# Attention's reciprocals turned with its maxima and spread over partitions by way of DRAM, in a hybrid encoder block

## The chip, the cores and the metric

The kernel runs on one core of a Trainium2 chip. The core has five engines with a queue of instructions each: TensorE (PE; its weight loads are listed as PEld), VectorE (DVE), ScalarE (ACT), GpSimd (POOL) and SyncE (SP), which here issues most DMAs. Each queue is worked off in order. The metric is the device time of one execution in microseconds, the median of the runs.

## The reference

One layer of an encoder over 2048 positions of width 1024, in float32:

```
h = rms_norm(x);  z = h @ W_in                       # 8 gated-MLP heads, 8 attention heads of 64
A = u * (W_s @ layer_norm(v) + b)                    # in blocks of 128 positions, masked
s = q @ k.T / 8 + c[t] - c[s],  s <= t               # c: running sum of log sigmoid(forget logits)
B = softmax(s) @ v                                   # per head
x = x + concat(A, B) @ W_out
x = x + (silu(conv(g)) * conv(val)) @ W_down         # [g, val] = rms_norm(x) @ W_up, causal width 3
out = rms_norm(x)
```

## The kernel before, in words

A float32 product is made of three products in the float32r type: each operand is split into a high and a low part, and high by high, high by low and low by high are summed in one PSUM bank (`mm3`, lines 203 to 213). These dense matmuls, 512 columns wide, are most of the work.

**Attention** runs as a generator beside them (`b_stream`, lines 684 to 703). It goes through four blocks of 512 queries (`tb`), and in each through eight heads (`h`). For one head there are two passes.

- `b_max` (lines 732 to 790) makes the scores of 128 queries by 512 keys (L752, L753), takes their maxima (L756, L758) and, with ScalarE, the sums of the exponentials (L761). At its end DVE makes the maximum over all keys, split in two parts (`m8`, 128 queries x 8: four groups of queries by high and low), and the reciprocals of the sums (`rr`, 128 x 4, L780 or L782).
- Its inner function `turn` (lines 784 to 788) turns `m8` on PE into 8 rows of 128 queries (L786), and DVE writes them, each in its own place by a mask of ones and zeros (`rowsel`), into rows 96 to 103 of the query tile `t1` (L787). With those rows in the product the second pass subtracts the maximum inside the matmul.
- `b_mix` (lines 792 to 851) makes the scores once more, now with the keys on partitions (L813, L814), their exponentials (L819), the split of those (L824, L825), and their product with the values (L801, L802) into one PSUM bank `o`. The two parts of the result are added into `op` (L836, L837), which holds an even head on partitions 0 to 63 and the odd head after it on 64 to 127.

The second pass of a head comes after the first pass of the next, and calls the next head's `turn` at its fourth group of 128 keys (`TURN` = 3). After an odd head the pair is divided by its sums: ScalarE widens the reciprocals of both heads to `rw`, 128 queries x 4 groups x 2 heads x 64 (L842); the generator yields; PE turns `rw` with four transposes of 128x128 (L844, whose matmuls stand in the helper `transpose4`, L183) into a score bank; and DVE multiplies `op` by it (L845). `op` is split and stored to the DRAM tensors `mixh` and `mixl` (L848 to L851), from which the output projection loads its rows (`load_mix`, lines 854 to 860).

**What orders the work.** Each dense matmul counts a tick (`tick`, lines 105 to 113); every 3.5 to 4.4 ticks, by the stage, the generator makes one step up to its next `yield`. `defer(n, fn)` calls `fn` n ticks later. `need(tb)` (lines 136 to 142) runs the generator on until a block of queries is finished. What comes out is a list with priorities (steps of the generator are raised by 100), and the framework's scheduler makes of it, before the run, a fixed order of instructions for each engine. Waits between engines and DMAs are semaphores, set by that order. A load that reads what a store wrote to DRAM waits, in the queue that issues it, until the store has landed. DMAs by `self.dma` are issued by SP, line 100.

**Buffers around the change.** `t1` and the key tile `m1` have two buffers each, `t2` two, `op` and `rw` one, `o` one bank, and score tiles take turns over three banks (five from the feed-forward stage on).

Of the kernel before, what the change touches and what calls it, by code (L numbers as in the profile page):

```python
# [8 lines left out]
F32 = mybir.dt.float32  # L9
F32R = mybir.dt.float32r  # L10
BF16 = mybir.dt.bfloat16
AF = mybir.ActivationFunctionType
ALU = mybir.AluOpType
# [5 lines left out]
P = 128  # L19
# [33 lines left out]
def f32(ap):  # L53
    return ap.bitcast(F32)
# [26 lines left out]
class Block:  # L81
# [134 lines left out]
    def constants(self):  # L216
        nc, a, tc = self.nc, self.a, self.tc
        cp = self.cpool = self.ctx.enter_context(tc.tile_pool(name="const", bufs=1))
        self.ident = cp.tile([P, P], F32, name="ident")
        make_identity(nc, self.ident)  # L220
        self.mhalf = cp.tile([P, 8], F32, name="mhalf")
        nc.gpsimd.memset(self.mhalf, -0.5)
        self.cols = cp.tile([P, 200], F32, name="cols")
        self.halo = cp.tile([P, 2 * NF, 2], F32, name="halo")
        cp.tile([P, 56], F32, name="even")
        nc.gpsimd.memset(self.halo, 0.0)
        dp = self.ctx.enter_context(tc.tile_pool(name="dram", bufs=1, space=DRAM))
        self.ones_d = dp.tile([2, HALF], F32, name="ones_d")
        t = lambda n, k, s: [dp.tile(s, F32, name=f"{n}{i}") for i in range(k)]
        self.qx = t("qx", 2, [8, 128, HALF])  # L230
        self.kx = t("kx", 2, [8, 132, HALF])
        self.cc = t("cc", 2, [8, 2, HALF])
        self.vd = t("vd", 2, [HALF, 8, P])
        self.mixh = t("mixh", 4, [D, TB])
        self.mixl = t("mixl", 4, [D, TB])
        self.rows_d = [t(f"rows{i}_", 8, [P, D]) for i in range(2)]
        self.act_d = [t(f"act{i}_", NF, [P, HALF]) for i in range(2)]
        self.tw_d = t("tw", NF // 2, [P, 2, D])

    def columns(self):  # L240

# [409 lines left out]
    def b_consts(self):  # L651
        nc, bp = self.nc, self.bp
# [15 lines left out]
        nc.gpsimd.affine_select(out=self.maskT, in_=self.maskT, compare_op=ALU.is_ge, fill=BIG, base=0,  # L668
                                pattern=[[1, P]], channel_multiplier=-1)

        self.rowsel = bp.tile([8, 4, P], BF16, name="rowsel")
        nc.gpsimd.memset(self.rowsel, 1.0)
        for base, mult in ((0, 1), (1, -1)):
            nc.gpsimd.affine_select(out=self.rowsel, in_=self.rowsel, compare_op=ALU.is_ge, fill=0.0, base=base,
# [9 lines left out]
    def b_stream(self, pieces):  # L684

        todo = None
        for h, tb in pieces:
            if tb >= 2 and not self.ready:
                if todo:
                    yield from self.b_mix(*todo, None)  # L690
                    self.done += 1
                    todo = None
                while not self.ready:
                    yield
            t1, t2, turn = yield from self.b_max(h, tb)
            if todo:
                yield from self.b_mix(*todo, turn)
                self.done += 1
            else:
                turn()  # L700
            todo = (h, tb, t1, t2, self.rr)
        yield from self.b_mix(*todo, None)
        self.done += 1

# [27 lines left out]
    def b_max(self, h, tb):  # L732

        nc, bp, pp = self.nc, self.bp, self.bpp
        hf, sl = tb // 2, slice((tb % 2) * TB, (tb % 2 + 1) * TB)
        self.T1.append(self.T1.pop(0))
        t1 = self.T1[0]
        t2 = self.til(self.mp, [P, TB], F32R, "t2")
# [2 lines left out]
        self.dma(f32(t2), self.qx[hf][h, :, sl])  # L741
        nm = self.til(bp, [P, 4, 4], F32, "part")
        ls = self.til(bp, [P, 4, 4], F32, "ls")
        if h % 2 == 0:
            self.rr = self.til(bp, [P, 4, 2], F32, "rr")
        for sb in range(tb + 1):
            m1, m2 = self.b_keys(h, sb, False)
            for tt in range(4):
# [16 lines left out]
            nc.vector.tensor_reduce(mx, nm[:, :, 0:tb + 1], axis=AX.X, op=ALU.min)  # L765
        else:
            nc.vector.tensor_copy(mx, nm[:, :, 0])
        m8 = self.til(bp, [P, 4, 2], F32R, "m8")
        nc.vector.tensor_scalar(m8[:, :, 0], mx, -1.0, None, ALU.mult)
        nc.vector.scalar_tensor_tensor(m8[:, :, 1], mx, -1.0, f32(m8[:, :, 0]), op0=ALU.mult, op1=ALU.subtract)  # L770
        rr = self.rr[:, :, h % 2]
        if tb:
            k = slice(0, tb + 1)
            lw = self.til(bp, [P, 4, 4], F32, "lw")
# [7 lines left out]
            nc.vector.reciprocal(rr, ls[:, :, 0])  # L782

        def turn():
            pm = self.scores([8, P])
            nc.tensor.transpose(pm, f32(m8).rearrange("p a b -> p (a b)"), self.ident)  # L786
            nc.vector.tensor_tensor(t1[96:104, :].rearrange("p (a b) -> p a b", a=4),  # L787
                                    pm.unsqueeze(1).broadcast_to([8, 4, P]), self.rowsel, op=ALU.mult)

        return t1, t2, turn  # L790

    def b_mix(self, h, tb, t1, t2, rr, turn):

        nc, bp, pp = self.nc, self.bp, self.bpp
        po = self.til(pp, [P, TB], F32, "o")
# [8 lines left out]
        for sc in range(ns):  # L804
            if sc == TURN and turn:
                turn()
            if sc % 4 == 0:
                m1, m2, v4 = self.b_keys(h, sc // 4, True)
            j = max(0, sc - 4 * tb)
# [24 lines left out]
        op = self.op  # L834
# [3 lines left out]
        if h % 2 == 0:  # L838
            return

        rw = self.til(self.mp, [P, 4, 2, 64], F32, "rw")
        nc.scalar.activation(rw, rr.unsqueeze(3).broadcast_to([P, 4, 2, 64]), AF.Copy)  # L842
        yield
        pr = self.transpose4(None, "s", [rw[:, i, :, :].rearrange("p a b -> p (a b)") for i in range(4)])  # L844
        nc.vector.tensor_tensor(op, pr, op, op=ALU.mult)  # L845
        oh = self.room([P, TB], F32R, "ph")
        ol = self.room([P, TB], F32R, "pl")
        self.split_sb(op, oh, ol)  # L848
# [669 lines left out]
```

## Time and profile before

| | us |
|---|---|
| median of 3 runs | 2418.84 |
| lowest and highest run | 2418.55, 2419.08 |
| the profiled execution | 2421.7 |
| its span (first to last instruction) | 2420.0 |
| PE busy in it | 2401.1 |
| DVE, ACT, POOL busy | 1757.0, 1352.3, 315.2 |

The stages of one execution: projections and gate, with attention's first blocks beside them, to about 600 us; the output projection, and the feed-forward of the first 1024 positions with the last two blocks of attention, to about 1500 us; then the feed-forward of the other 1024 positions. In a row of a timeline stand the start, the length, engine, line, operation, the output and inputs by the program's names without buffer numbers, and the shape; in a row by line the count, the busy time and the mean of one in ns, then the idle time of the engine just before with what ended it; in a row of waits who waited for whom, the sum, how often, and the longest. A matmul's bar begins before the one ahead of it has ended, so that bars overlap; the distance between starts is what each takes from the others.

### The profile page before, as it was taken

To read this page: it belongs to the slowest core of one execution; us is meant where nothing else is said; L and a number is where in the kernel's file an instruction comes from. 1 tells how busy PE (TensorE), PEld (TensorE's weight loads), DVE (VectorE), ACT (ScalarE), POOL (GpSimd) and SP (SyncE) were. 2 spreads that over 40 slices of the span, in tenths; PEclk is the share of its full clock that TensorE was granted. 3 is DMA by queue.
4 is the path that set the end of the run, shared out by engine and by line. 5 is a ranking of instruction groups with operands and counts; after the bars stand their busy time and mean duration, and the time that the engine had idled before them with its cause. 6 is when DMAs were issued, how large, how long until landed. Compare 5 with 4: busy or idle time off the path is not lost.

```text
span 2420.0 us, 32601 instructions
## 1 busy us (share of the span) xinstructions
PE 2401.1 (99%) x10984; PEld 1980.9 (82%) x10984; DVE 1757.0 (73%) x3086; ACT 1352.3 (56%) x2635; POOL 315.2 (13%) x303
## 2 busy tenths in 40 slices
PE   9999999999999999999999999999999999999998
PEld 7788888788888888888887888888888888888887
DVE  5448775565568778878778775598888877857776
ACT  4347766554446555767676764465555455454443
POOL 3114140000242111111111101100000000000000
PEclk9999999999999999999999999999999999999999
DMA  8853636658755444555445555312222228538633
GB/s 294 274 142 120 202 113 180 168 171 268 261 189 182 161 162 161 164 172 184 148 151 180 165 196 197 126 53 89 86 79 87 87 91 315 160 100 297 205 118 122
DMA packets 245031, 400.51 MB, mean 165 GB/s; under 512 B 51240, under 2 KB 109736, under 8 KB 243440
## 3 DMA queue, kind: packets, MB, share of 16 engines
q1 hardware_dynamic: 239824, 374.31, 48.3%
q0 software_dynamic: 5040, 24.12, 2.6%
q8 instruction: 87, 1.43, 0.2%
q14 instruction: 80, 0.66, 0.1%
HBM read 304.76 MB, written 93.72 MB: 165 GB/s over the span
## 4 chain that ended last, share of the span: by engine, by line
PE 93%; DMA 2%; DVE 2%; ACT 1%; issue 1%; POOL 0%; SPq 0%; DVEq 0%; POOLq 0%; ACTq 0%
PE D L1358 15%; PE mm L212 14%; PE mm L210 14%; PE mm L208 14%; PE A L1156 3%; PE A L1157 3%; PE A L1158 3%; PE o L802 2%; PE o L801 2%; PE s L753 2%; PE s L752 2%; PE s L814 2%; PE s L813 2%; PE B L1157 2%; PE B L1158 2%; PE B L1156 2%
## 5 line engine op out<-in xcount | busy, mean ns | idle before, releaser
L210 PE MATMUL mm<-tlo,whi 128*128 128x512 f32 x912 | 357.9, 392 | 0.0
L212 PE MATMUL mm<-thi,wlo 128*128 128x512 f32 x912 | 357.2, 392 | 0.0
L208 PE MATMUL mm<-thi,whi 128*128 128x512 f32 x912 | 356.8, 391 | 0.0
L150 POOL TENSOR_SCALAR whi<-raw 128x1024 fp32r<-128x1024 f32 (+1 forms) x112 | 128.5, 1148 | 978.8 <-PE mm L210 624.3
L212 PE MATMUL mm<-whi,tlo 128*128 128x512 f32 x640 | 251.5, 394 | 1.5 <-DMA tlo<-mixl 1.5
L208 PE MATMUL mm<-whi,thi 128*128 128x512 f32 x640 | 251.9, 395 | 0.0
L210 PE MATMUL mm<-wlo,thi 128*128 128x512 f32 x640 | 250.9, 393 | 0.1
L761 ACT ACTIVATE s<-s,part 128x512 f32<-128x512 f32 (+3 forms) x261 | 154.7, 593 | 145.5 <-DVE part L756 88.5
L208 PEld LDWEIGHTS mm<-thi,whi 128*128 128x128 f32 x912 | 171.4, 188 | 35.5
L825 DVE TENSOR_TENSOR pl<-e,ph 128x512 fp32r<-128x512 f32 (+1 forms) x218 | 145.7, 677 | 75.1 <-ACT ph L824 42.5
L210 PEld LDWEIGHTS mm<-tlo,whi 128*128 128x128 f32 x912 | 171.5, 188 | 34.4
L212 PEld LDWEIGHTS mm<-thi,wlo 128*128 128x128 f32 x912 | 171.5, 188 | 34.4
L819 ACT ACTIVATE e<-s 128x512 f32<-128x512 f32 (+1 forms) x222 | 113.9, 530 | 106.0 <-DVE s L817 49.8
L162 DVE TENSOR_TENSOR wlo<-raw,whi 128x1024 fp32r<-128x1024 f32 x104 | 136.0, 1308 | 48.3 <-POOL whi L150 48.2
L824 ACT ACTIVATE ph<-e 128x512 fp32r<-128x512 f32 (+1 forms) x218 | 120.2, 563 | 43.5 <-PE o L801 40.2
L1358 PE MATMUL D<-wl,xh 128*128 128x512 f32 x368 | 141.3, 389 | 0.0
L1358 PE MATMUL D<-wh,xh 128*128 128x512 f32 x368 | 140.8, 389 | 0.2 <-DVE xo L1436 0.2
L212 PEld LDWEIGHTS mm<-whi,tlo 128*128 128x128 f32 x640 | 120.3, 188 | 25.2 <-DMA tlo<-mixl 1.8
L210 PEld LDWEIGHTS mm<-wlo,thi 128*128 128x128 f32 x640 | 120.4, 188 | 23.6 <-DVE wlo L162 0.5
L208 PEld LDWEIGHTS mm<-whi,thi 128*128 128x128 f32 x640 | 120.4, 188 | 23.3
L1358 PE MATMUL D<-wh,xl 128*128 128x512 f32 x368 | 137.2, 389 | 0.0
L756 DVE TENSOR_REDUCE part<-s 128x1 f32<-128x512 f32 x149 | 98.5, 683 | 27.8 <-PE s L753 26.9
(1860 smaller groups left out, 5836.5 us busy)
## 6 DMA issues: line engine op xcount, KB each, us to landing
raw<-in_w_up_dram SPq DMA_DIRECT2D x72, 512.0 KB
m<-kx SPq DMA_DIRECT2D x134, 256.0 KB
m<-kx SPq DMA_DIRECT2D x160, 136.0 KB
x<-act SPq DMA_DIRECT2D x84, 256.0 KB
raw<-in_w_in_dram SPq DMA_DIRECT2D x36, 512.0 KB
v<-vd SPq DMA_DIRECT2D x67, 256.0 KB
raw<-in_w_out_dram SPq DMA_DIRECT2D x24, 512.0 KB
tw<-in_w_down_dram SPq DMA_DIRECT2D x11, 1024.0 KB
```

The source lines that it names most:

```text
L150: self.cast_ins = self.nc.gpsimd.tensor_scalar(out, in_, 1.0, 0.0, ALU.mult, ALU.add).ins
L162: nc.vector.tensor_tensor(lo, raw, f32(hi), op=ALU.subtract)
L208: mm(ps, lhsT=ah[k], rhs=bh[k], start=k == 0, stop=False)
L210: mm(ps, lhsT=ah[k], rhs=bl[k], start=False, stop=False)
L212: self.last_mm = mm(ps, lhsT=al[k], rhs=bh[k], start=False, stop=k == n - 1).ins
L761: nc.scalar.activation(ps[:, :n], ps[:, :n], AF.Exp, scale=-1.0, bias=dst, accum_out=ls[:, tt, sb:sb + 1])
L824: nc.scalar.activation(ph[:, c], e[:, c], AF.Copy)
L825: nc.vector.tensor_tensor(pl[:, c], e[:, c], f32(ph[:, c]), op=ALU.subtract)
L1156: mm(ps, lhsT=xh[:, ks], rhs=yh[:, k, :], start=fresh and k == 0, stop=False, **kw)
L1157: mm(ps, lhsT=xh[:, ks], rhs=yl[:, k, :], start=False, stop=False, **kw)
L1158: mm(ps, lhsT=xl[:, ks], rhs=yh[:, k, :], start=False, stop=k == 3, **kw)
L1358: nc.tensor.matmul(bank[t], lhsT=x[i][:, ts], rhs=w[k], start=fresh and j == 0 and i + k == 0, stop=last and i == 1, **kw)
```

## The change

`m8` grows from 8 to 12 columns (`m12`): the four columns of reciprocals stand behind the eight of the maxima, and `rr` is now that part of the tile. `turn` makes one transpose of 12 columns; DVE writes the eight rows into `t1` as before, and then copies all twelve rows from PSUM to one of three places in the unused partitions of the mask's tile (`turned_rows`). The four rows of reciprocals, 512 bytes each, are stored 14 ticks later to a DRAM tensor of the pair (`rl_d`, 16 of them, 2 heads x 4 x 128). In the odd head's second pass, at its second group of keys, two loads bring them back, each head's 2 KB to all 64 partitions of that head (`rl`, in the buffer that `rw` had). The product of L845 then reads `rl` from SBUF. The widening on ScalarE, the four transposes, the yield ahead of them and the turned tile in a score bank are gone.

```
@@ constants
+        self.rl_d = t("rl", 16, [2, 4, P])
@@ b_consts
-        self.rowsel = bp.tile([8, 4, P], BF16, name="rowsel")
+        sel = bp.tile([P, 4, P], BF16, name="rowsel")
+        self.rowsel = sel[0:8]
+        self.turned_rows = [sel[i:i + 12].rearrange("p a b -> p (a b)")[:, 0:256].bitcast(F32) for i in (32, 64, 96)]
@@ b_max
-        if h % 2 == 0:
-            self.rr = self.til(bp, [P, 4, 2], F32, "rr")
...
-        m8 = self.til(bp, [P, 4, 2], F32R, "m8")
+        m12 = self.til(bp, [P, 12], F32R, "m8")
+        m8 = m12[:, 0:8].rearrange("p (a b) -> p a b", b=2)
...
-        rr = self.rr[:, :, h % 2]
+        rr = f32(m12[:, 8:12])
...
         def turn():
-            pm = self.scores([8, P])
-            nc.tensor.transpose(pm, f32(m8).rearrange("p a b -> p (a b)"), self.ident)
+            pm = self.scores([12, P])
+            nc.tensor.transpose(pm, f32(m12), self.ident)
             nc.vector.tensor_tensor(t1[96:104, :].rearrange("p (a b) -> p a b", a=4),
-                                    pm.unsqueeze(1).broadcast_to([8, 4, P]), self.rowsel, op=ALU.mult)
+                                    pm[0:8, :].unsqueeze(1).broadcast_to([8, 4, P]), self.rowsel, op=ALU.mult)
+            self.turned_rows.append(self.turned_rows.pop(0))
+            pc = self.turned_rows[0]
+            nc.vector.tensor_copy(pc, pm)
+            self.defer(14, lambda: self.dma(self.rl_d[4 * tb + h // 2][h % 2], pc[8:12, :]))
@@ b_mix
         for sc in range(ns):
             if sc == TURN and turn:
                 turn()
+            if sc == 1 and h % 2:
+                rl = self.til(self.mp, [P, 4, P], F32, "rw")
+                for i in range(2):
+                    self.dma(rl[64 * i:64 * i + 64, :, :], self.rl_d[4 * tb + h // 2][i:i + 1, :, :].broadcast_to([64, 4, P]))
...
-        rw = self.til(self.mp, [P, 4, 2, 64], F32, "rw")
-        nc.scalar.activation(rw, rr.unsqueeze(3).broadcast_to([P, 4, 2, 64]), AF.Copy)
-        yield
-        pr = self.transpose4(None, "s", [rw[:, i, :, :].rearrange("p a b -> p (a b)") for i in range(4)])
-        nc.vector.tensor_tensor(op, pr, op, op=ALU.mult)
+        nc.vector.tensor_tensor(op, rl.rearrange("p a b -> p (a b)"), op, op=ALU.mult)
```

In the three places where the order of instructions is shown below, names carry their buffer numbers.

More of the change, by code (lines that the diff above doesn't have):

```diff
@@ L700, in b_stream @@
                 turn()
-            todo = (h, tb, t1, t2, self.rr)
+            todo = (h, tb, t1, t2)
         yield from self.b_mix(*todo, None)
@@ L784, in turn, with b_mix @@
         def turn():
-            pm = self.scores([8, P])
-            nc.tensor.transpose(pm, f32(m8).rearrange("p a b -> p (a b)"), self.ident)
+            pm = self.scores([12, P])
+            nc.tensor.transpose(pm, f32(m12), self.ident)
             nc.vector.tensor_tensor(t1[96:104, :].rearrange("p (a b) -> p a b", a=4),
-                                    pm.unsqueeze(1).broadcast_to([8, 4, P]), self.rowsel, op=ALU.mult)
+                                    pm[0:8, :].unsqueeze(1).broadcast_to([8, 4, P]), self.rowsel, op=ALU.mult)
[3 more added lines that the diff above has]
+            self.defer(14, lambda: self.dma(self.rl_d[4 * tb + h // 2][h % 2], pc[8:12, :]))
         return t1, t2, turn
-    def b_mix(self, h, tb, t1, t2, rr, turn):
+    def b_mix(self, h, tb, t1, t2, turn):
         nc, bp, pp = self.nc, self.bp, self.bpp
```

## The prediction

> **What bounds the kernel now.** I read the page first, then the stages, then who made TensorE (PE) wait, then the timeline around the removed work. Every row is of the kernel before.
>
> ```profile
> PE 2401.1 (99%) x10984; PEld 1980.9 (82%) x10984; DVE 1757.0 (73%) x3086; ACT 1352.3 (56%) x2635; POOL 315.2 (13%) x303
> DMA packets 245031, 400.51 MB, mean 165 GB/s; under 512 B 51240, under 2 KB 109736, under 8 KB 243440
> PE 93%; DMA 2%; DVE 2%; ACT 1%; issue 1%; POOL 0%; SPq 0%; DVEq 0%; POOLq 0%; ACTq 0%
> ```
>
> The first row says that PE works nearly all of the span, the third that 93% of the chain that ends last is PE work. So a microsecond of PE work taken out is worth about a microsecond, as long as PE does not wait longer elsewhere. Attention, where the change sits, runs from about 130 to 1500 us. The stages (columns: length, then PE busy with its instructions, PEld, DVE, ACT, POOL, PE clock, DMA share, GB/s):
>
> ```profile
> 130.00:480.00 350.00, 349.61 (x1729) 291.67 (x1728) 237.40 (x493) 225.24 (x425) 80.39 (x48) 1.00 0.54 157
> 480.00:790.00 310.00, 307.61 (x1439) 251.67 (x1437) 200.81 (x386) 157.49 (x343) 61.17 (x60) 1.00 0.66 213
> 790.00:1500.00 710.00, 708.39 (x3221) 586.53 (x3220) 550.89 (x1074) 463.03 (x1018) 119.48 (x108) 1.00 0.52 169
> ```
>
> PE idles 0.39 + 2.39 + 1.61 = 4.39 us in these 1370 us, at a full granted clock; DVE is busy 989 us, 72%. The list of PE's waits names nearly all of the 4.39 us:
>
> ```profile
> PE mm L212 <- DMA tlo<-mixl: 1.5, 1, 1.5
> PE s L752 <- DMA t<-qx: 0.9, 1, 0.9
> PE s L753 <- DMA t<-qx: 0.7, 1, 0.7
> PE s L752 <- DMA t<-cc: 0.5, 1, 0.5
> PE dn L752 <- DMA t<-cc: 0.2, 1, 0.2
> ```
>
> All are loads by SP: once the mixed rows of query block 1, and in four heads of 32 the queries of the next head (0.9 + 0.7 + 0.5 + 0.2 = 2.3 us). SP is therefore the only other queue that PE feels.
>
> **Part 1: 64 transposes leave PE.** Each pair of heads turned the widened reciprocals (`rw`) with four transposes.
>
> ```profile
> L183 PE MATMUL s<-ident,rw x60: 270/272/299, 188.0 to 1476.7; 128*128 128x128 f32 x60
> L183 PE MATMUL dn<-ident,rw x4: 272/273/279, 1285.2 to 1285.7; 128*128 128x128 f32 x4
> ```
>
> These 272 ns are bars of a pipeline, not time taken from the neighbours. What four cost is read from starts. Two places, in the timeline of PE (start, length):
>
> ```profile
> 1285.15 0.39 PE L183 MATMUL dn<-ident,rw 128*128 128x128 f32 x2
> 1285.30 0.48 PE L801 MATMUL o<-ph+_2776_11742,v+_2769_11718 128*128 128x512 f32 x1
> 1285.61 0.38 PE L183 MATMUL dn<-ident,rw 128*128 128x128 f32 x2
> 1285.75 0.48 PE L802 MATMUL o<-pl+_2777_11743,v+_2769_11718 128*128 128x512 f32 x1
> 1286.07 0.40 PE L210 MATMUL mm<-tlo,whi 128*128 128x512 f32 x1
> 1286.30 0.39 PE L212 MATMUL mm<-thi,wlo 128*128 128x512 f32 x1
> ...
> 1390.90 0.22 PE L813 MATMUL s<-t,m 128*128 128x128 f32 x1
> 1390.96 0.28 PE L814 MATMUL s<-t,m 128*128 128x128 f32 x1
> 1391.08 0.41 PE L183 MATMUL s<-ident,rw 128*128 128x128 f32 x2
> ...
> 1392.01 0.40 PE L802 MATMUL o<-pl+_3027_12773,v 128*128 128x512 f32 x1
> ```
>
> A 512-column matmul takes 1286.30 - 1286.07 = 0.23 us of PE. The first place lasts 1286.07 - 1285.15 = 0.92 us and holds two of them, so the four transposes cost 0.92 - 0.46 = 0.46 us. The second lasts 1392.01 - 1391.08 = 0.93 us, also with two (L801 and L212), so 0.47; and the 128-column matmul ahead of it took 0.12 us where its twin took 0.06, so at most 0.53. Over 16 pairs that is 7.4 to 8.5 us; I take the middle, 0.495, so **-7.9 us**. Nothing hides it: PE is the chain here.
>
> The order of PE at the first pair of heads (`o_284` is the product with the values of its second head, `rw_306` the widened reciprocals, `mm_325` and `mm_326` the same output tile of the gate). Before:
>
> ```order
> L212 MATMUL mm_325_1818<-whi_215_1426,tlo_25_296 128x512
> L208 MATMUL mm_325_1818<-whi_215_1426,thi_23_294 128x512
> L210 MATMUL mm_325_1818<-wlo_216_1427,thi_23_294 128x512
> L183 MATMUL s_307_1774<-ident_58,rw_306_1769 128x128 x2
> L801 MATMUL o_284_1682<-ph_299_1727,v_286_1686 128x256
> L183 MATMUL s_307_1774<-ident_58,rw_306_1769 128x128 x2
> L212 MATMUL mm_325_1818<-whi_215_1426,tlo_25_296 128x512
> L208 MATMUL mm_351_1921<-whi_206_1408,thi_22_293 128x512
> ```
>
> and with the change (line numbers run up to 10 higher):
>
> ```order
> L212 MATMUL mm_326_1839<-whi_215_1442,tlo_25_312 128x512
> L208 MATMUL mm_352_1940<-whi_206_1424,thi_22_309 128x512
> L807 MATMUL o_284_1700<-ph_300_1748,v_286_1704 128x256
> L210 MATMUL mm_352_1940<-wlo_207_1425,thi_22_309 128x512
> L753 MATMUL s_314_1807<-m1_52_411,t1_54_413 128x128
> L753 MATMUL s_315_1816<-m1_52_411,t1_54_413 128x256
> ```
>
> The transposes are gone and nothing has come in their place; the next score matmuls move up behind the gate's.
>
> **Part 2: work of DVE and ACT.**
>
> ```profile
> L842 ACT ACTIVATE rw<-rr 128x512 f32<-128x512 f32 x16 | 10.1, 632 | 2.9 <-DVE rr L780 2.5 <-DVE rr L782 0.3
> L845 DVE TENSOR_TENSOR op<-s,op 128x512 f32<-128x512 f32 x15 | 10.3, 688 | 0.3
> L817 DVE TENSOR_TENSOR s<-s,maskT 128x128 f32<-128x128 f32 x108 | 30.0, 292 | 19.5 <-PE s L814 19.1
> L600 DVE COPY fs<-tp x4: 180/182/192, 44.8 to 490.8; 128x32 f32<-128x32 f32 x4
> ```
>
> ACT loses 16 widenings, 10.1 us. The product with `op` (688 ns) stays. DVE gains 32 copies of 12x128 from PSUM; no row shows that form. The nearest are the mask addition over 128 columns (292 ns) and a PSUM copy of 32 columns (182 ns): 5.8 to 9.3 us, say 8, since the free length is that of the dearer row. They fit into DVE's 381 idle us of the stages, and each stands behind the product that writes the query tile, so the score matmuls do not wait for it. The turn keeps its one transpose, with 12 columns for 8, and still streams the 128 columns of the identity. I cost all of part 2 at nothing on PE; without that cover the copies would cost their 8 us.
>
> **Part 3: 64 DMAs enter SP's queue**, 32 stores of 2 KB and 32 loads of 128 KB. The loads carry 4.2 MB beside 400.51 MB, about 1%. What issuing costs SP, and how long transfers were under way where the chain passed through them:
>
> ```profile
> 993.49 0.45 SPq L100 DMA_DIRECT2D t<-qx  x1
> 994.00 0.43 SPq L100 DMA_DIRECT2D t<-cc  x1
> 994.52 0.32 SPq L100 DMA_DIRECT2D t<-qx  x1
> ...
> ```
>
> ```profile
> 653.48 4.33 DMA mixl<-pl
> 657.88 7.25 DMA tlo<-mixl
> 726.51 7.63 DMA t<-qx
> 994.00 5.83 DMA t<-cc
> ```
>
> 64 issues at 0.32 to 0.45 us are 20 to 29 us of SP time, spread over 1370 us. The dear thing is the wait: a load waits on SP until its store has landed, and SP issues in order. The order of SP at the twelfth head, an odd one (`rl5` is its pair's buffer in DRAM; `t1` and `t2` are the queries of the next head, `m1` and `m2` keys, `v` values). Before:
>
> ```order
> L100 DMA m1_53_396<-kx0_74 68x512
> L100 DMA m2_877_3803<-kx0_74 128x512
> L100 DMA v_895_3904<-vd0_78 128x4x128
> L100 DMA t1_55_398<-qx0_72 64x512
> L100 DMA t1_55_398<-cc0_76 2x512
> L100 DMA t2_873_3796<-qx0_72 128x512
> ```
>
> and with the change:
>
> ```order
> L100 DMA m1_53_412<-kx0_74 68x512
> L100 DMA m2_867_3783<-kx0_74 128x512
> L100 DMA rl5_164<-rowsel_407 4x128
> L100 DMA rw_900_3909<-rl5_164 64x512
> L100 DMA t1_55_414<-qx0_72 64x512
> L100 DMA t1_55_414<-cc0_76 2x512
> L100 DMA t2_864_3777<-qx0_72 128x512
> ```
>
> Here the load stands directly behind its store, and the next head's queries, exactly the loads for which PE waited above, stand behind both. In the 16 odd heads the load follows its own store within one to six rows, in ten of them at once. The even head's load stands nine rows or more behind its store, but for four pairs with one or two.
>
> How long SP is held: no row shows a 2 KB store. Nearest is the 256 KB store of `mixl`, whose dependent load could go 4.33 us after the issue; the least is nothing but the issue. 32 holds of 4.33 us would be 139 us of SP. What reaches PE is less, because loads are issued ahead: the query load of 7.63 us made PE wait 0.9 us and that of 5.83 us made it wait 0.5, so the order leaves 5.3 to 6.7 us between such an issue and its use. The bounds for PE are -2.9 us (4.39 less the 1.5 counted below: all other waits vanish, as the order is made anew) and 32 x 0.9 = 28.8 us. I take the trace's own sum for query loads once more, **+2.3 us**, near the lower end, since today's 32 heads with these cuts waited in only four cases.
>
> The Trainium skill, DMA: Bandwidth & Descriptors, section Anatomy of one DMA, gives a fixed cost of about 2.0 us per DMA, mostly the receipt of the write, heaviest for HBM. By that, an estimate, a store would hold SP about 2 us instead of up to 4.33, and the sum would be that without new waits, 2409.4; no run here shows it yet.
>
> Does DVE wait for `rl`? In the tightest pair, from the odd head's turn to the product:
>
> ```profile
> 159.68 0.68 DVE L787 TENSOR_TENSOR t<-s,rowsel 8x512 fp32r<-8x512 f32 x1
> ...
> 192.46 0.69 DVE L845 TENSOR_TENSOR op<-s,op 128x512 f32<-128x512 f32 x1
> ```
>
> That is 32.8 us. The new path needs 14 ticks (14 x 0.23 = 3.2 us, somewhat more with attention's own matmuls between), a store (4.33) and a load (7.63): some 15 us. It is hidden with room for the queue; if it came late, DVE would stand at the product and its scores' reductions behind it.
>
> **Part 4: one step less per pair.** The generator no longer yields ahead of the transposes, so attention runs ahead of the dense matmuls by some matmuls a pair. That matters where mixed rows are awaited, the 1.5 us at `tlo<-mixl`. SP's order there (`mixh1` and `mixl1` are the mixed rows of block 1, `rows0_n` the finished row blocks of the output projection). Before:
>
> ```order
> L100 DMA rows0_3_91<-acc_1377_6100 128x1024
> L100 DMA mixh1_81<-ph_1248_5240 128x512
> L100 DMA mixl1_85<-pl_1249_5241 128x512
> L100 DMA acc_1560_6795<-in_x_dram 128x1024
> L100 DMA thi_1435_6387<-mixh1_81 128x2x512
> L100 DMA tlo_1437_6389<-mixl1_85 128x2x512
> ```
>
> and with the change:
>
> ```order
> L100 DMA mixh1_81<-ph_1246_5210 128x512
> L100 DMA mixl1_85<-pl_1247_5211 128x512
> L100 DMA m2_1420_6291<-kx0_74 128x512
> L100 DMA rows0_1_89<-acc_1375_6104 128x1024
> L100 DMA thi_1435_6396<-mixh1_81 128x2x512
> L100 DMA tlo_1437_6398<-mixl1_85 128x2x512
> ```
>
> The last pair's store and the load behind it now stand two row blocks earlier. A row block is 24 matmuls of 0.23 us, 5.5 us, so about 11 us are won against a wait of 1.5: it goes, **-1.5 us**. Late next on that path is the query load, already counted.
>
> **The sum** against the profiled execution: span 2420.0 - 7.9 - 1.5 + 2.3 = 2412.9; the execution's own 2421.7 becomes 2414.6. The median of the three runs is 2418.84, 2.9 below it, and those runs lie within 0.6 us of each other, so the same -7.1 us gives **2411.7**.
>
> **The rivals.** One measurement of this kernel can tell about 0.2% (4.8 us) from no change: below 2414.0 is faster, above 2423.7 slower.
>
> *The holds eat the gain.* PE waits 0.5 us (the `t<-cc` row) in each of the 16 odd heads: -9.4 + 8.0, 2417.4. For it speaks the order of SP above; against it that before only four of 32 heads waited at all. Chance 0.20.
>
> *Slower.* Behind both loads of a pair PE waits as long as in its worst case before, 0.9 us: 32 x 0.9 = 28.8, so 2418.8 - 9.4 + 28.8 = 2438.2. The place is SP at the loads of `rl`. It decides from 9.4 + 4.8 = 14.2 us of new waits, 0.44 us a head. Against it: most even heads' stores have long landed, and SP's longest waits are for PE to free a buffer, time that can absorb a hold (columns: sum, times, longest):
>
> ```profile
> SPq L100 <- PE s L753: 206.5, 69, 9.6
> SPq L100 <- PE s L814: 162.8, 55, 11.4
> ```
>
> Chance 0.08.
>
> *The bars are real.* If a transpose held PE for its bar of 272 ns, 64 would give 17.4 us, so 2418.8 - 17.4 - 1.5 + 2.3 = 2402.2. Against it: at 1285.15 two of them and the start of the next matmul lie within 0.15 us. Chance 0.02. The Trainium skill, TensorE: Matmul & The Clock Gate, section Part 4: PE-mode transpose, gives about 275 ns for one in a kernel; the trace agrees with the length of the bar, but not as a cost in a pipeline.
>
> **How the numbers follow.** 0.70 stays for the forecast, whose own range is 2418.8 - 8.5 - 4.4 = 2405.9 to 2414.0. The range of 8 in 10 goes up to the first rival's 2417.4, leaving out the slower case, the bars and the worst of the middle. Faster 0.70 + 0.02 = 0.72, same 0.20, slower 0.08.
>
> **What would show it.** PE busy down by about 8 us with 64 matmuls fewer; no PE wait for `tlo<-mixl`; in SP's waits new entries for `rl`, each of 2 to 4 us; PE's waits for `t` and `m` together near 4 to 5 us; DVE's copies at 0.2 to 0.3 us; no DVE wait of note for `rw`. The prediction is wrong if PE waits behind SP for more than 5 us beyond today's, if DVE stands at the product, or if PE busy falls by less than 7 us.

## The result, and the profile after

| | before | after |
|---|---|---|
| median, 14 runs each | 2420.74 us | 2424.77 us |
| lowest to highest | 2418.55 to 2424.32 | 2421.68 to 2428.66 |
| profiled execution, its span | 2421.7, 2420.0 | 2421.68, 2419.9 |

The ratio is 1.0015, with an interval of 1.0008 to 1.0022: about 3.6 us slower, less than the 0.2% that counts as a difference. The forecast was 7.1 us faster, and the result lies above its range. Its base was low too: the first three runs of before had a median of 2418.84, 1.9 us below the median of all. The profiled execution of after was the quickest of its runs. A second one, profiled later, has a span of 2423.8 us.

The page of after, busy time, DMA total and chain:

```profile
PE 2396.9 (99%) x10920; PEld 1975.3 (82%) x10920; DVE 1760.8 (73%) x3118; ACT 1339.4 (55%) x2619; POOL 318.0 (13%) x303
DMA packets 247848, 404.77 MB, mean 167 GB/s; under 512 B 51880, under 2 KB 110504, under 8 KB 246256
PE 83%; DMA 3%; DVE 2%; ACT 1%; issue 1%; POOL 0%; SPq 0%; DVEq 0%; POOLq 0%; ACTq 0%
```

PE has 64 matmuls fewer, as announced, but its busy time fell by 4.2 us only, and the span by 0.1. PE's share of the chain fell from 93% to 83%. The stages of after:

```profile
130.00:480.00 350.00, 345.83 (x1692) 286.38 (x1691) 240.20 (x493) 219.85 (x418) 80.88 (x48) 1.00 0.56 160
480.00:790.00 310.00, 309.47 (x1441) 253.28 (x1440) 202.78 (x405) 159.34 (x353) 58.75 (x59) 1.00 0.66 215
790.00:1500.00 710.00, 708.14 (x3204) 586.28 (x3203) 550.59 (x1088) 454.94 (x1000) 123.60 (x109) 1.00 0.52 173
```

PE's idle time in the first stage is 4.17 us, where before had 0.39. The clock is full in both, so it is not the clock. PE's waits in after:

```profile
PE mm L425 <- POOL whi L150: 1.9, 1, 1.9
PE s L823 <- DMA m<-kx: 1.4, 1, 1.4
PE s L753 <- DMA t<-qx: 1.1, 2, 0.8
PE s L753 <- ACT s L762: 1.1, 1, 1.1
PE s L754 <- DMA t<-qx: 0.9, 2, 0.7
PE o L808 <- DVE pl L835: 0.8, 2, 0.4
PE s L753 <- DMA t<-cc: 0.4, 1, 0.4
```

The wait for `tlo<-mixl` is gone. The query loads stand at 1.1 + 0.9 + 0.4 = 2.4 us, as before (2.3). New are a key load (`m<-kx`), the exponentials of ACT and the split of DVE: three different releasers, a DMA and two engines. (The wait of L425 lies at 8 us, ahead of attention, and varies from run to run.) SP's new waits in after:

```profile
SPq L100 <- DVE rowsel L793: 49.8, 16, 10.3
SPq L100 <- DMA rl<-rowsel: 46.3, 15, 5.5
SPq L100 <- DVE op L851: 32.7, 9, 5.8
```

The second row is the hold that the prediction described: the load stands until its store has landed, 15 times, 46.3 / 15 = 3.1 us in the mean. The first is a hold that it did not see, the store waiting for DVE's copy. Nor did it see the third, the load waiting for the product of the pair before, because `rl` has one buffer.

**One such hold, followed to PE.** SP of after near the end of attention, start and length of each issue:

```profile
1433.67 0.26 SPq L100 DMA_DIRECT2D rl<-rowsel  x1
1439.50 0.45 SPq L100 DMA_DIRECT2D rw<-rl  x1
1440.05 0.90 SPq L100 DMA_DIRECT2D m<-kx  x2
```

and PE of after just behind it:

```profile
1442.26 0.39 PE L212 MATMUL mm<-thi,wlo 128*128 128x512 f32 x1
...
1443.17 0.39 PE L208 MATMUL mm<-thi,whi 128*128 128x512 f32 x1
1444.94 0.47 PE L823 MATMUL s<-t,m 128*128 128x512 f32 x1 [1.38 <-DMA m<-kx]
```

The store is issued at 1433.67, the load behind it only at 1439.50, the keys behind both at 1440.05. PE needs the keys at 1443.4 and gets them at 1444.94.

**Counting PE's waits.** The list says 1.38 us, but the distance of the last two starts is 1.77 us, and a 512-column matmul takes (1443.17 - 1442.26) / 4 = 0.2275 us (three stand between the two); so 1.54 us are lost. A bar of 0.39 us covers the first 0.16 us of any wait, and busy time therefore counts short waits as work. In what follows I use the time from the first matmul's start to the last one's (some 10 us less than the span) less the columns of all matmuls, at 0.2275 / 512 us a column (twice that where the identity is an operand; four transposes are then 0.455 us, as the prediction's rows gave). I call the rest **not streaming**; it is what PE lost, wherever it was lost. By it, the 64 transposes are 7.3 us of work; before did not stream for 41.7 us of its span, after for 48.9, its second profile for 52.8. So 7.2 to 11.1 us of new losses stand against the saving of 7.3. One profile is one execution: in those used here it lay from 3.1 us below the median of its kernel (after) to 3.5 us above (without transfers, with yield), so a figure of one profile is good to some 3 us, and the ratios, which rest on all runs, decide.

### The profile page after: what moved, and what is told of

It is laid out like the page before. It is cut to its first block, busy times and chain, and to the rows that moved or that the text cites. A ratio compares the mean times of both kernels' runs of the same rounds, so it can differ in the third digit from the quotient of the medians.

```text
span 2419.9 us, 32553 instructions
## 1 busy us (share of the span) xinstructions
PE 2396.9 (99%) x10920; PEld 1975.3 (82%) x10920; DVE 1760.8 (73%) x3118; ACT 1339.4 (55%) x2619; POOL 318.0 (13%) x303
## 4 chain that ended last, share of the span: by engine, by line
PE 83%; DMA 3%; DVE 2%; ACT 1%; issue 1%; POOL 0%; SPq 0%; DVEq 0%; POOLq 0%; ACTq 0%
PE D L1364 16%; PE mm L210 11%; PE mm L212 11%; PE mm L208 11%; PE A L1162 3%; PE A L1164 3%; PE A L1163 3%; PE o L808 2%; PE o L807 2%; PE s L754 2%; PE s L753 2%; PE s L824 2%; PE s L823 2%; PE B L1163 2%; PE B L1164 2%; PE B L1162 2%
## 5 line engine op out<-in xcount | busy, mean ns | idle before, releaser
L150 POOL TENSOR_SCALAR whi<-raw 128x1024 fp32r<-128x1024 f32 (+1 forms) x112 | 128.5, 1148 | 951.5 <-PE mm L210 532.4
L762 ACT ACTIVATE s<-s,part 128x512 f32<-128x512 f32 (+3 forms) x261 | 154.5, 592 | 151.5 <-DVE part L757 109.3
L835 DVE TENSOR_TENSOR pl<-e,ph 128x512 fp32r<-128x512 f32 (+1 forms) x219 | 142.3, 658 | 68.6 <-PE o L808 40.4
L162 DVE TENSOR_TENSOR wlo<-raw,whi 128x1024 fp32r<-128x1024 f32 x104 | 140.1, 1348 | 61.6 <-POOL whi L150 61.3
```

Of the source, the lines that this page charges most:

```text
L150: self.cast_ins = self.nc.gpsimd.tensor_scalar(out, in_, 1.0, 0.0, ALU.mult, ALU.add).ins
L162: nc.vector.tensor_tensor(lo, raw, f32(hi), op=ALU.subtract)
L762: nc.scalar.activation(ps[:, :n], ps[:, :n], AF.Exp, scale=-1.0, bias=dst, accum_out=ls[:, tt, sb:sb + 1])
L835: nc.vector.tensor_tensor(pl[:, c], e[:, c], f32(ph[:, c]), op=ALU.subtract)
```

## The experiments

All ratios are to the kernel before, timed on the same chip. The spans and the two last columns (us) are of one profile each. "300 to 360" is the part of the loss that falls between 300 and 360 us of the span. "Transfers" are the stores and loads of `rl`.

| kernel | transposes a pair | transfers | ratio (interval) | span | not streaming | 300 to 360 |
|---|---|---|---|---|---|---|
| before | 4 | none | | 2420.0 | 41.7 | 3.5 |
| before, no yield | 4 | none | 0.9999 (0.9990 to 1.0008) | 2419.2 | 40.9 | 3.5 |
| before, pace up | 4 | none | 1.0011 (1.0002 to 1.0020) | 2420.7 | 42.4 | 3.8 |
| before, pace down | 4 | none | 1.0009 (1.0000 to 1.0018) | 2423.1 | 44.8 | 3.6 |
| before, 8 transposes | 8 | none | 1.0051 (1.0039 to 1.0064) | 2429.5 | 43.9 | 4.2 |
| before, no transposes | 0 | none | 0.9989 (0.9980 to 0.9998) | 2414.3 | 43.2 | 2.9 |
| after, no transfers | 0 | none | 0.9991 (0.9982 to 1.0000) | 2416.6 | 45.3 | 7.3 |
| the same, with yield | 0 | none | 1.0004 (0.9996 to 1.0013) | 2422.5 | 51.5 | 7.5 |
| after, no transfers, no copies | 0 | none | 1.0005 (0.9996 to 1.0013) | 2420.5 | 49.5 | 6.5 |
| after, stores only | 0 | stores | 0.9997 (0.9988 to 1.0005) | 2417.2 | 46.2 | 8.3 |
| after, loads only | 0 | loads | 0.9988 (0.9979 to 0.9997) | 2416.8 | 45.8 | 4.7 |
| after | 0 | both | 1.0015 (1.0008 to 1.0022) | 2419.9 | 48.9 | 6.4 |
| after, again | 0 | both | 1.0021 (1.0012 to 1.0031) | 2423.8 | 52.8 | 7.7 |
| after, all by GpSimd | 0 | both | 1.0005 (0.9996 to 1.0013) | 2419.8 | 48.7 | 6.9 |
| after, stores by GpSimd | 0 | both | 1.0011 (1.0002 to 1.0020) | 2421.4 | 50.3 | 7.5 |
| after, loads by GpSimd | 0 | both | 1.0028 (1.0017 to 1.0040) | 2427.1 | 56.0 | 8.1 |
| after, queries first | 0 | both | 1.0028 (1.0017 to 1.0038) | 2428.1 | 57.1 | 6.8 |
| after, pace up | 0 | both | 1.0032 (1.0020 to 1.0043) | 2425.3 | 54.2 | 6.9 |
| after, with yield | 0 | both | 1.0041 (1.0027 to 1.0054) | 2432.0 | 60.9 | 7.1 |
| before, with transfers | 4 | both | 1.0101 (1.0085 to 1.0117) | 2441.7 | 63.3 | 9.1 |

PE's waits can also be parted by what ended them. These are sums, in us, of the waits that PE's lists show between 130 and 1500 us (the first 0.16 us of each is missing, as said):

| kernels | for loads | for ACT, DVE, GpSimd |
|---|---|---|
| before | 3.8 | 0.3 |
| three other orders with 4 transposes, no transfers | 0 to 2.9 | 0.5 to 1.6 |
| before, 8 transposes | 2.2 | 2.4 |
| four kernels with neither transposes nor transfers | 1.5 to 2.4 | 3.9 to 6.9 |
| after, stores only; loads only | 2.8; 0.8 | 3.6; 2.6 |
| after; after, again | 3.8; 5.6 | 2.5; 5.4 |
| six other kernels without transposes, with both transfers | 2.1 to 7.5 | 3.4 to 7.3 |

In all 14 profiles without the transposes PE waits more for the other engines (2.5 to 7.3 us) than in the five that have them and no transfers (0.3 to 2.4). With both transfers the loads mostly come on top.

### Do the holds cost the gain, or the new order?

Theory H was that SP's holds bring the loads behind them late to PE; its rival O, that the new order of instructions has other waits. After once more:

> The changed kernel again, for a second profile: ratio 1.0008 to 1.0022 as before. Both theories expect PE waits of a few us beyond the kernel before; theory H expects them behind loads that SP issued after a hold, at the same places as in the first profile.

1.0021, as measured at first. In this profile PE waits for keys (`m<-kx`) four times, 2.8 us in all. Three of the four, at 1096, 1310 and 1449 us, were loads that SP issued 0.5 to 2.7 us behind a load of `rl` for which it had stood; the last is the place of the first profile, as H expects. Then after without stores and loads; the copies stay, and the product reads a constant tile, so that the division is left out:

```diff
-            self.defer(14, lambda: self.dma(self.rl_d[4 * tb + h // 2][h % 2], pc[8:12, :]))
-            if sc == 1 and h % 2:
-                rl = self.til(self.mp, [P, 4, P], F32, "rw")
...
-        nc.vector.tensor_tensor(op, rl.rearrange("p a b -> p (a b)"), op, op=ALU.mult)
+        nc.vector.tensor_tensor(op, self.rl, op, op=ALU.mult)
```

> The changed kernel without its stores and loads of reciprocals: the product with op takes a constant tile of ones, so the division by attention's sums is left out. Transposes, widening and the yield stay gone, the copies stay. If the held queue costs the gain (theory H: SP stands at loads that wait for their stores to land, 46 us in 15 waits, and what is queued behind comes late for TensorE), this is 8 to 10 us below the kernel before, ratio 0.996 to 0.997. If the new order of instructions costs it (theory O: each edit that moves the attention steps makes another order, whose waits differ by some us, whatever the DMAs do), it is within 0.998 to 1.002.

0.9991, within O's range and not H's. The transfers, with what they change in the order, cost 0.0024 to 0.0030, 6 to 7 us. But without them only 2.2 us of the 7.3 appear: some 5 us are lost with no hold for `rl` in the program. So each theory has about one half of the loss on its side. The waits of this kernel lie partly at the same places as those of after. From its PE list:

```profile
PE o L809 <- DVE pl L832: 1.6, 2, 1.2
PE s L755 <- ACT s L764: 1.5, 2, 1.2
PE s L756 <- DMA t<-qx: 1.1, 1, 1.1
```

The other way round, the copies, stores and loads were put into before, which keeps widening, transposes and yield (the loads go into the buffer that the widening then overwrites):

```diff
@@ before, turn and b_mix
+            nc.vector.tensor_copy(pc, pm)
+            self.defer(14, lambda: self.dma(self.rl_d[4 * tb + h // 2][h % 2], pc[4:8, :]))
...
+            if sc == 1 and h % 2:
+                rl = self.til(self.mp, [P, 4, P], F32, "rw")
...
+        rw = rl.rearrange("p a (b c) -> p a b c", b=2)
```

> The kernel before with the change's copies, stores and loads added, and the widening, the transposes and the yield all kept. The loads fill the buffer that the widening writes over afterwards, so their values are not used; what is stored are four rows of the maxima. Theory H: slower by what the queue costs, 8 to 12 us, ratio 1.003 to 1.005. Theory O: within 0.9985 to 1.0015.

1.0101, 24 us, far more than either theory expected. This kernel has a wait that after has not: ScalarE must let the load land before it widens into the same buffer, and its queue stands there.

```profile
ACT rw L853 <- DMA rw<-rl: 52.4, 15, 7.3
```

So its 24 us are not the price of the transfers in after, and it settles nothing on H.

Then all 64 DMAs from GpSimd's queue (`nc.gpsimd.dma_start` for `self.dma`):

> The changed kernel with its 64 stores and loads issued by GpSimd instead of SP, so that SP never stands at a load of reciprocals. Theory H: 7 to 9 us below the kernel before, ratio 0.9965 to 0.997, unless GpSimd's weight casts are held in turn. Theory O: 0.999 to 1.002, like the changed kernel.

1.0005: between, better than after by 0.0010 to 0.0016, and within O's range, not H's.

### What of the order?

Three candidates: the missing yield (Y), the 32 copies (C), or no single edit (R). After with the yield put back ahead of the product:

> The kernel after, with the yield ahead of the product put back (nothing else). Three theories for the part of the lost gain that stays without the DMAs. Y: the missing step moves attention against the dense matmuls, and that makes the new waits; C: the 32 copies keep the turn's score bank and DVE longer; R: no single edit, any new order of instructions has its own waits, a few us more or less. By Y the waits of about 5 us go: ratio to before 0.999 to 1.0003. By C and R it stays near that of after: 1.0005 to 1.003.

The same without transfers:

> The kernel after without the stores and the loads (product with a constant tile of ones, so the division is left out; copies kept) and with the yield put back. By Y the full 7.3 us of the removed transposes show: ratio 0.9965 to 0.998. By C and R no gain over the kernel without DMAs and without the yield: 0.9982 to 1.000.

Without transfers and without `nc.vector.tensor_copy(pc, pm)`:

> The kernel after without stores, loads and the 32 copies (product with a constant tile of ones, so the division is left out). By C the full 7.3 us show: ratio 0.9965 to 0.998. By Y and R it stays near the kernel that keeps the copies: 0.9983 to 1.000.

And before with only its `yield` taken out:

> The kernel before, with only the yield ahead of the four transposes removed. By Y slower by about 5 us: ratio 1.0015 to 1.0035. By C the same: 0.9995 to 1.0005. By R anything from 0.9985 to 1.003, the sign not known beforehand.

1.0041, 1.0004, 1.0005 and 0.9999. Y falls three times: putting the yield back makes it slower, and taking it out of before changes nothing. C falls: without copies it is not faster. What is left is R, though the first three lie even above the ranges given for it; it is what remains, not what was shown. So I shifted the order with the same instructions, by the pace of attention (ticks a step):

```diff
-RATES = [3.5, 4.0, 4.4, 3.6]
+RATES = [3.6, 4.1, 4.5, 3.7]
```

That is "pace up" in the table; "pace down" has 3.4, 3.9, 4.3, 3.5.

> The kernel before with the same instructions, and attention's pace changed a little: 3.6, 4.1, 4.5, 3.7 ticks a step for 3.5, 4.0, 4.4, 3.6. Theory T: the settings of before suit the order that they give, and another order of the same work has more waits on PE, some 4 to 12 us: ratio 1.0015 to 1.005. Theory S: the orders without the transposes lose for a reason of their own, and before does not care for a small shift: 0.999 to 1.001.

> The kernel before with attention's pace changed the other way: 3.4, 3.9, 4.3, 3.5 ticks a step. By T 1.0015 to 1.005, by S 0.999 to 1.001.

> The kernel after with the pace of 3.6, 4.1, 4.5, 3.7 ticks a step. By T the kernel after has no settings of its own yet, so a shift may go either way: from 0.9975 (the gain comes out) to 1.004. By S it stays at 1.0005 to 1.003.

1.0011, 1.0009 and 1.0032. Before loses some 2.5 us in both directions (1.0009 is in S's range, 1.0011 between S and T), and after another 3 to 4. The yield, too, moves the same instructions only: taken out of before it was worth 0.2 us, put back where it was missing it cost 3 to 6. A shift of the order alone is thus worth up to 6 us here, most often 2 to 4, where 7.3 were to be had, and none of the shifts tried gained clearly.

### Is PE's time at this place worth its length?

Before without the four transposes (the product reads `rw` unturned, so the division is left out), and before with each four made twice:

```diff
-        pr = self.transpose4(None, "s", [rw[:, i, :, :].rearrange("p a b -> p (a b)") for i in range(4)])
-        nc.vector.tensor_tensor(op, pr, op, op=ALU.mult)
+        nc.vector.tensor_tensor(op, rw.rearrange("p a b c -> p (a b c)"), op, op=ALU.mult)
@@ the other kernel, behind transpose4
+        for i in range(4):
+            nc.tensor.transpose(pr[:, i * P:(i + 1) * P], rw[:, i, :, :].rearrange("p a b -> p (a b)"), self.ident)
```

> The kernel before without the four transposes of a pair; widening, yield and everything else are kept, and the product reads the widened reciprocals as they are (not turned, so the division is left out). Linear theory: each four transposes are worth 0.46 us of the end, ratio 0.9965 to 0.998. Theory W: whatever order comes out without them has new waits of PE for other engines that take most of it back: 0.9983 to 1.0008.

> The kernel before with the four transposes of a pair made twice, into the same score bank (64 more of them on PE, 7.4 us by the starts of the trace; same result). Linear theory: ratio 1.0025 to 1.0045. If PE's time at this place were hidden behind another limit: 0.999 to 1.0015. More than 1.0045 would be new waits on top.

PE's row of the page, of the kernel without transposes:

```profile
PE 2393.1 (99%) x10920; PEld 1973.2 (82%) x10920; DVE 1754.7 (73%) x3086; ACT 1347.5 (56%) x2635; POOL 316.5 (13%) x303
```

and of the one with eight:

```profile
PE 2410.6 (99%) x11048; PEld 1987.8 (82%) x11048; DVE 1757.7 (72%) x3086; ACT 1350.3 (56%) x2635; POOL 314.9 (13%) x303
```

Sixty-four more cost 0.0051, 12.3 us, more than their 7.3; sixty-four fewer gave 0.0011, 2.7 us (0.5 to 4.8), in the profiled execution 5.7. So PE's time does count, and work put on PE is paid in full. Work taken off is paid back in part only, as theory W of the expectation has it. W's new waits are in PE's list of the kernel without transposes, where before has none for ACT's exponentials in attention:

```profile
PE s L752 <- ACT s L761: 3.2, 4, 1.3
```

### Which part of the transfers?

First, the loads behind the next head's query loads in SP's order (`issue_after` the load of `t2`; the stores stay where they were):

> The kernel after, with the two loads of rl put behind the next head's query loads in SP's order (the stores stay ahead of them). By the theory that SP's stand at the load, with the queries behind it, is the dear part of the DMAs, most of their 6 to 7 us come back: ratio 0.999 to 1.0002, like the kernel without the DMAs. If the stores' wait for DVE's copy, or the traffic, or the order of instructions is the dear part: 1.001 to 1.003.

SP's waits in this kernel:

```profile
SPq L100 <- DVE rowsel L799: 65.9, 17, 10.3
SPq L100 <- DMA rl<-rowsel: 23.5, 5, 5.6
```

The hold for the landing was halved, 46.3 to 23.5 us, while the one for the copies grew from 49.8 to 65.9, and the time rose to 1.0028. Then stores alone and loads alone:

> The kernel after with its copies and stores, without the loads (product with a constant tile of ones, so the division is left out). If the stores, for which SP waits until DVE has copied, are the dear part of the DMAs: near the kernel after, 1.001 to 1.0025. If the loads are: near the kernel without DMAs, 0.9982 to 1.0002.

> The kernel after with its copies and the 32 loads, without the stores; the loads read rows of ones that were stored at the start, so they wait for no store (the division is left out). If the loads' traffic or place in SP's queue is the dear part, or their wait for the buffer: 1.001 to 1.0025. If the stores, or the loads' wait for the stores, are: 0.9982 to 1.0002.

0.9997 and 0.9988, against 0.9991 without either. SP's wait in the one,

```profile
SPq L100 <- DVE rowsel L795: 49.1, 16, 10.2
```

and in the other:

```profile
SPq L100 <- DVE op L850: 27.5, 9, 4.5
```

So the 49 us that SP stands for DVE's copies cost some 1.5 us by the ratios, which is within their intervals, and its stand for the buffer nothing, nor do 4.2 MB more of traffic. Only both together are dear, and what comes with both is the load's wait for its store. The order of PE hardly takes part in this: matched by operands and shapes, after and the kernel with the stores alone differ in the place of 23 of their 10920 matmuls, after and the kernel without transfers in 139. The kernel with the loads alone differs in 979, so it is the weaker comparison. Two kernels put one side of it on GpSimd's queue:

> The kernel after with only the 32 loads of rl issued by GpSimd (the stores stay with SP), so that GpSimd and not SP stands until a store has landed. Stores alone measured 0.9997, loads alone 0.9988, both 1.0015 to 1.0021. If SP's stand at the load is what makes both dearer than each: near the stores alone, 0.999 to 1.0006. If the order or the traffic of both is, or GpSimd's stand costs as much: 1.001 to 1.0025.

> The kernel after with only the 32 stores issued by GpSimd (the loads stay with SP, which still stands until the store has landed, but no longer waits for DVE's copies). If SP's stand at the load is the dear part: near the kernel after, 1.001 to 1.0025. If the wait for the copies is: 0.999 to 1.0006.

1.0028 and 1.0011; the second is what was expected if SP's stand at the load is the dear part. With the loads on GpSimd, GpSimd stands instead, and far longer than SP did:

```profile
POOL rw L816 <- DMA rl<-rowsel: 152.1, 14, 37.9
```

and PE waits for GpSimd's `ar`, which in after it does not:

```profile
PE dn L183 <- POOL ar L899: 1.9, 1, 1.9
```

The stand may be harmful in that queue as well, then; that this wait comes of it was not followed. With the stores on GpSimd, SP still stands for the landing (54.0 us, 16 times, 5.8 at the longest), and the time falls only to 1.0011. No place for the transfers gave back all that they cost. Each of these moves also makes the order of PE anew: against after some 900 matmuls change their place with the queries first or the stores on GpSimd, some 2000 with the loads or both there. With 2 to 4 us for a shift of the order alone, the ratios of these four kernels can't be put down to the holds alone.

No kernel that computes the whole layer beat before.

## Why the prediction was wrong

**The step that failed** is the term of +2.3 us for new waits, with the sentence ahead of it that a microsecond off PE is worth one "as long as PE does not wait longer elsewhere". PE did wait longer elsewhere, 7.2 and 11.1 us in the two profiles of after. The term looked only at one queue (SP) and one kind of victim (query loads), and just these stayed at 2.4 us in the first profile (2.8 in the second). In their place came waits for ACT, DVE and GpSimd (2.5 and 5.4 us listed, 0.3 before) and for keys (1.4 and 2.8 us, none before). That SP is "the only other queue that PE feels" was read from a list that left out one row of the same view, already a wait for an engine:

```profile
PE o L802 <- DVE pl+_2781_11758 L825: 0.3, 1, 0.3
```

Of the three signs of being wrong that the prediction named, one came: PE busy fell by less than 7 us.

**Part 1, -7.9 us.** The work was sized nearly rightly: 7.3 us by columns. (Busy time fell by less than the 8 us announced, 4.2; bars cover the first part of each new wait.) What was wrong is "nothing hides it". With the transposes away and no transfers at all, the times were 0.9989, 0.9991, 1.0004 and 1.0005: 2.7 us won to 1.2 lost instead of 7.3 won. PE not streaming rose from 40.9 to 44.8 us in the four orders with four transposes to 43.2 to 51.5 in these four.

A part of that has a place. Between 300 and 360 us all six kernels that keep the widening on ScalarE and have no transfers lose 2.9 to 4.2 us; all that have no widening lose 4.7 to 8.3. In after PE waits there for query loads, at 303 to 305 and at 340 us, and for ACT at 350 us. The kernel without transfers has waits for query loads at 303 and 337 us and for ACT at 347 us as well, so the holds for `rl` are not needed for them. The wait for ACT in after can be followed. ACT:

```profile
339.96 0.59 ACT L846 ACTIVATE op<-o 64x512 f32<-64x512 f32 x1
346.99 1.06 ACT L567 ACTIVATE vn<-ln 128x1024 f32<-128x1024 f32 x1 [6.45 <-DVE ln L564]
348.07 1.28 ACT L762 ACT_TABLE_LOAD   x1
349.37 0.66 ACT L762 ACTIVATE s<-s,part 128x512 f32<-128x512 f32 x1
```

DVE, on which L567 waits:

```profile
338.46 4.28 DVE L162 TENSOR_TENSOR wlo<-raw,whi 128x1024 fp32r<-128x1024 f32 x2
342.67 1.21 DVE L562 TENSOR_REDUCE lns<-ln 128x16 f32<-128x1024 f32 x1
...
344.65 0.70 DVE L847 TENSOR_TENSOR op<-o,op 64x512 f32<-64x512 f32 x1
345.38 1.52 DVE L564 TENSOR_TENSOR ln<-ln,lns 128x1024 f32<-128x1024 f32 x1
```

GpSimd beside it:

```profile
338.41 1.04 POOL L150 TENSOR_SCALAR whi<-raw 128x1024 fp32r<-128x1024 f32 x1 [1.14 <-DVE ln L575]
339.42 4.48 POOL L577 TENSOR_TENSOR vn<-ln,lng 128x512 f32<-128x512 f32 x2
```

and PE:

```profile
348.53 0.39 PE L208 MATMUL mm<-whi,thi 128*128 128x512 f32 x1
348.76 0.39 PE L210 MATMUL mm<-wlo,thi 128*128 128x512 f32 x1
350.20 0.50 PE L753 MATMUL s<-m,t 96*128 96x512 f32 x1 [1.05 <-ACT s L762]
```

Read it from the end. PE waits 1.05 us for a score bank that the exponential of L762 frees. The exponential stands in ACT's queue behind L567, the squares of the gate's norm, and ACT stands idle 6.45 us at that one. L567 waits for DVE's L564, and DVE works without a gap from 338.46 us up to it; that stretch is long because its two weight splits (L162) take 4.28 us together, beside GpSimd's cast (L150) and its products (L577). Between L567 and the exponential ACT also loads a table, 1.28 us, more than PE's whole wait; in before the table load ahead of an exponential stands at 332.29 us, with no wait of PE behind it. In before DVE has a split alone there:

```profile
338.67 1.21 DVE L162 TENSOR_TENSOR wlo<-raw,whi 128x1024 fp32r<-128x1024 f32 x1
340.00 1.21 DVE L563 TENSOR_TENSOR ln<-ln,lns 128x1024 f32<-128x1024 f32 x1
```

and ACT does L566, as the line is numbered there, nearly 6 us earlier, ahead of the exponentials instead of late in front of them:

```profile
341.25 1.06 ACT L566 ACTIVATE vn<-ln 128x1024 f32<-128x1024 f32 x1 [0.51 <-DVE ln L563]
346.22 0.66 ACT L761 ACTIVATE s<-s,part 128x512 f32<-128x512 f32 x1 [1.84 <-DVE part L756]
```

None of these instructions is in the diff. The change took work from PE and ACT, the scheduler made another order, and in it other work meets. That the widening's removal, which the prediction costed at nothing, is what brings this place about follows only from the grouping of the kernels; it was not tried alone. The kernel without transposes that keeps the widening has no such loss here, but others at 790 to 1500 us (14.0 against 10.9); among them are two waits for ACT's exponentials, 0.99 us at 944 and 1.35 us at 1166 us. Whether PE, having less to do, must meet the other engines more often, or whether these orders are just less lucky than that of before, was not separated; fourteen profiles against five speak for the first, without proving it.

**Part 2** was right in what it names: the copies take 0.28 us, and PE does not wait for them.

```profile
L793 DVE COPY rowsel<-s 12x128 f32<-12x128 f32 x28 | 7.8, 278 | 0.3
```

**Part 3** had the hold at up to 4.33 us; it was 3.1 in the mean, 5.5 at the longest. The Trainium skill, DMA: Bandwidth & Descriptors, section Anatomy of one DMA, gives its fixed cost of about 2.0 us for the DMAs that GpSimd issues. These stores were issued by SP, and the trace is above that figure in the mean; the measurement decides. The holds for the copies and for the buffer were not foreseen, but where each stood alone the runs showed it to be nearly free. That the product does not wait for `rl` was right:

```profile
L851 DVE TENSOR_TENSOR op<-rw,op 128x512 f32<-128x512 f32 x16 | 11.6, 725 | 0.3
```

The transfers cost 6 to 7 us together. The prediction's bounds for PE (-2.9 to 28.8 us) held that, the value chosen from them, +2.3, was about a third of it. It argued from the four of 32 heads that waited before; the delay went to key loads instead, as at 1444.94 us.

**Part 4** was right that the wait for `tlo<-mixl` goes, but not shown right in its reason. The wait is in no other profile either, also not where the yield stays (before with another pace, with eight transposes or with none). Taking out the yield alone gave 0.9999: 1.5 us (0.06%) is less than that interval can show.

**The rivals.** "The holds eat the gain", at 0.9994 of before, named the mechanism that the stores and loads alone point to for one half, though with query loads where keys were hit; it lacked the other half. "Slower" expected 0.9 us in every head, which did not come. "The bars are real" expected 17.4 us for 64 transposes; 64 more of them cost 12.3 us, new waits included.

## What to carry to other kernels

Where a scheduler sets the order, an edit that takes work off the bounding engine also makes a new order everywhere, and the new order's waits are a term of the sum: measure its size by shifting the order of the unchanged kernel a little (here some 2.5 us), and do not count on a gain of the same size. In a queue that works in order, ask of each instruction that may stand there what is behind it, and follow it over two or three engines (GpSimd to DVE to ACT to PE). A load that reads back what its own queue has just stored makes that queue stand; the stand is cheap where nothing behind it is urgent, and dear where keys or queries are.

## What the runs showed of the hardware

DVE and GpSimd hold each other up, and they do it by taking turns. The split of 1024 columns on DVE (L162), with two inputs in SBUF, took 1.20 to 1.23 us in all 239 cases in which GpSimd had no work of 512 or more columns beside it (before, after and after again). It took the same in all 38 cases in which it started ahead of GpSimd's instruction. Where GpSimd had started first, it took 1.90 to 2.32 us in 34 of 35 cases (in the other the starts lie 0.06 us apart). In the second profile of after:

```profile
785.66 1.29 POOL L980 TENSOR_TENSOR tw<-tw 128x512 f32<-128x512 f32 x1
785.72 2.31 DVE L162 TENSOR_TENSOR wlo<-raw,whi 128x1024 fp32r<-128x1024 f32 x1 [0.52 <-POOL whi L150]
```

GpSimd keeps its 1.29 us; DVE ends at 788.03, 1.08 us after it, as if it had begun its work only then. The other way round, in before, GpSimd's cast came 0.13 us behind DVE's L563 of 340.00 us, shown above; DVE kept its 1.21 us, and the cast took nearly twice the 1.05 us of the one before it:

```profile
340.13 2.01 POOL L150 TENSOR_SCALAR whi<-raw 128x1024 fp32r<-128x1024 f32 x1 [2.86 <-DMA raw<-in_w_in_dram]
```

When each has several such instructions they alternate, and all but the first are long, as DVE's two splits and GpSimd's two products at 338 to 344 us in after (4.28 and 4.48 us). DVE's split of 512 columns (L835) takes 0.68 us alone and up to 1.78 us so; in the second profile of after this made PE wait 1.71 us at 829 us. A reduction, with one input, kept its 1.21 us. The Trainium skill, GPSIMD Engine Reference, section 1. Specifications, says that GpSimd's SBUF interfaces are shared with VectorE, with contention for DVE instructions that have two SBUF inputs; the trace agrees.
